# A layer with PEER experts: when the expert rows are fetched, and into which buffers

## The chip, the cores and the metric

The kernel runs on one core of a Trainium2 chip, in one launch. The metric is the device time of that launch in microseconds (us), lower is better. Three runs of the kernel before gave 1982.49, 1975.41 and 1972.63 us, a median of 1975.41. The profiled execution took 1973.37 us, of which the profile's span is 1971.6.

## The reference, cut to what matters

One transformer layer over 512 latent tokens of width 1024 (with 256 context tokens as extra keys): modulated norm, projections, latent attention beside a convolution module, gates, an output projection; then modulated norm and the PEER experts, a residual and a last norm. The part that this change is about:

```python
q = (xc @ w_pq).reshape(P_CHUNK, P_HEADS, 2, P_DK // 2)        # 8 heads
s = jnp.einsum('thpd,hpkd->thpk', q, sub_keys)
s_top, i_top = lax.top_k(s, P_TOPK)                            # 16 of 128 keys, twice
...
expert = e1 * N_KEYS + e2                                      # 16 experts a head, of 16384
gate = jax.nn.softmax(best, axis=-1)
act = jax.nn.gelu(jnp.einsum('thkd,td->thk', u_tab[expert], xc))
return jnp.einsum('thk,thkd->td', gate * act, v_tab[expert])
```

So each token uses 8 x 16 = 128 rows of 1024 numbers from a table u, and 128 rows from a table v.

## The kernel before, in words

The 512 tokens are four tiles of 128, in two groups: tiles 0 and 1, and tiles 2 and 3. The groups go through the layer one after the other, and the experts of the two groups are computed in different ways.

**Group 0 gathers its rows.** For tile q (tile 0) and tile r (tile 1), `expert_in` (line 702) fetches one u row for each of the 128 tokens, 128 x 4 KB = 512 KB, by an indirect DMA that POOL issues (line 704), and DVE multiplies it with the tokens and sums (line 707). There are 128 such calls a tile; below, a *u row* is one such 128-token fetch. When all 128 products of q are there, `expert_mid` (line 724) applies gelu on ACT and the gates on DVE and has PE transpose weights and indices (lines 731, 732). Then `expert_out` (line 737) handles q's v rows in 32 *v groups*: four fetches of 512 KB each (line 748), and eight matmuls that accumulate in PSUM (line 753). For tile r the v rows are summed on DVE instead (`expert_sum`, lines 764 and 770).

**Group 1 computes all 16384 experts densely.** `dense` (from line 843) goes through 64 steps. A step loads two blocks of u and two of v (4 x 512 KB, by SP's DMA queue), splits each into a high and a low part (ACT line 94, DVE line 95), multiplies (PE lines 115 to 117), applies gelu once (ACT line 859) and the scattered gates (DVE line 862). Every eight blocks or so it loads a piece of the gates (`gr`).

**The two are interleaved.** `gathers` (line 774) lists group 0's calls in one fixed order: 128 u rows of q, the `expert_mid` of q, 48 u rows of r (NU = 48), 26 v groups of q, the other 80 u rows of r, the `expert_mid` of r, the last 6 v groups of q (LATE = 6), and 128 sums of r. While group 1 runs, `beside` (line 791) is called at fixed places and takes from that list at a fixed rate: 3.5 rows a unit of the second attention, 6 a column of the second merge (8 columns), 2 a chunk of its output projection, 6 a head of the second route, 0.4 a piece of the scatter of the gates, 4.1 a dense step. A v group counts as four rows. The stages of group 1 in the profile are, in us from the start of the span: second attention about 600 to 740, second merge 740 to 893, its output projection to 919, second route about 920 to 1070, scatter 1070 to 1184, dense 1184 to 1950.

**Buffers.** Every fetched row has a buffer of 4 KB a partition in the pool `gp`, tag `g`, six buffers. POOL issues its fetches in program order and each waits until the last reader of its buffer is done (DVE for a u row, PE for a v row), so six rows at most are on the way or unread. The tile framework orders each engine's instructions as the calls come, with small moves, and gives a buffer to a new tile only when the old tile's last reader stands earlier in the program.

**An idle piece.** `hh` (line 132) holds the modulated activations as a high part `hb0` and a low part `hb1`, each 8 KB a partition. The second group uses only the first (`hb[:1]`, lines 980 and 991), so the low part lies idle from then on.

The lines that decide which call waits for which buffer:

```python
g = gp.tile([P, D], F32, name="g", tag="g")        # expert_in, expert_out, expert_sum; GPB = 6
todo += us[:NU] + vs + us[NU:]                     # gathers: 48 u rows, 26 v groups, 80 u rows
todo += [(4, expert_out, q, i) for i in range(32 - LATE, 32)]
```

Of the kernel before, what the change touches and what calls it, by code (L numbers as in the profile page):

```python
# [8 lines left out]
F32 = mybir.dt.float32  # L9
BF16 = mybir.dt.bfloat16  # L10
F32R = mybir.dt.float32r
# [7 lines left out]
P = 128  # L19
D = 1024  # L20
KC = 8
# [24 lines left out]
PIECES, POFF = 1, 1  # L46
QPOS = (0, 0, 0)
GATES, GOFF, GSTEP = 4, 3, 6
LATE, N0, NU = 6, 0, 48

GROUPS = [[0, 1], [2, 3]]
GT = 2 * P
TB = 16
CB = 8
KEPT = (12,)


@with_exitstack
def tile_layer(ctx, tc, a, out):
    nc = tc.nc  # L60
    te, ve, se, ge, sy = nc.tensor, nc.vector, nc.scalar, nc.gpsimd, nc.sync
# [7 lines left out]
    ep = early.enter_context(tc.tile_pool(name="ep", bufs=1, side="right"))  # L69
# [58 lines left out]
    ones = consts.tile([P, P], F32)  # L128
    ve.memset(ones, 1.0)

    hb = [ep.tile([P, KC, GT], F32, name=f"hb{i}") for i in range(2)]
    hh = tuple(t.bitcast(F32R) for t in hb)
    ckvT = ep.tile([P, NKV], F32)
    KT = [[ep.tile([P if j else HD, NKV], F32, name=f"KT{i}{j}") for j in range(2)] for i in range(2)]
    rows = dram.tile([4, D], F32, name="rows")
# [1 line left out]
    hTd = dram.tile([P, KC, GT], F32, name="hTd")  # L137
# [128 lines left out]
    for i in range(6):  # L266
        t = big(f"x{i}")
# [3 lines left out]
    with tc.tile_pool(name="tmp0", bufs=1) as t0:  # L271
# [48 lines left out]
        for g, o in enumerate((hh, h2nd)):  # L320
            for q in range(2):
                ks = slice(4 * q, 4 * q + 4)
                v = hT[g][q]
# [50 lines left out]
    def queries(tiles, hx):  # L374

        cqT = sp.tile([P, 2, GT], F32, name="cqT", tag="sgm", bufs=2)
        QT = [[None, None] for _ in tiles]
        return QT, [lambda: query_in(tiles, hx, cqT)] + [lambda hf=hf: query_half(tiles, cqT, QT, hf) for hf in range(2)]
# [320 lines left out]
        ve.tensor_mul(gt, gt, mx[:, :, None].to_broadcast([P, PH, TOPK]))  # L699


    def expert_in(r, s):
        g = gp.tile([P, D], F32, name="g", tag="g")
        ge.indirect_dma_start(out=g, out_offset=None, in_=a["u"],  # L704
                              in_offset=bass.IndirectOffsetOnAxis(ap=r["ei"][:, s:s + 1], axis=0))
        scr = sp.tile([P, D], BF16, name="scu", tag="scu")
        ve.scalar_tensor_tensor(scr, g, 1.0, r["h2"], op0=ALU.mult, op1=ALU.mult, accum_out=r["act"][:, s:s + 1])  # L707
# [30 lines left out]
    def expert_out(r, i):  # L738
        if i == 0:
            r["acc"] = psV.tile([P, D], F32, name="acc")  # L740
        acc = r["acc"]
        z = Wz[i % 2]
        ve.tensor_copy(z[:, :, 31], r["wT"][:, i::32])
        gs = []
        for j in range(4):
            tk = 32 * j + i
            g = gp.tile([P, D], F32, name="g", tag="g")
            ge.indirect_dma_start(out=g, out_offset=None, in_=a["v"],  # L748
                                  in_offset=bass.IndirectOffsetOnAxis(ap=r["iT"][:, tk:tk + 1], axis=0))
            gs.append(g)  # L750
        for c in range(2):
            for j in range(4):
                te.matmul(acc[32 * j:32 * j + 32, 512 * c:512 * c + 512], z[:, j, 31 - i:63 - i],  # L753
                          gs[j][:, 512 * c:512 * c + 512], start=i == 0, stop=i == 31,
                          tile_position=(0, 32 * j))
        if i == 31:
            finish(acc, r["t"], lambda n: gp.tile([P, D], F32, name=n, tag="g"))
# [16 lines left out]
    def gathers(res):  # L774
        q, r = res
        todo = [(1, expert_in, q, s) for s in range(NSLOT)]
        todo.append((0, expert_mid, q))
        us = [(1, expert_in, r, s) for s in range(NSLOT)]
        vs = [(4, expert_out, q, i) for i in range(32 - LATE)]
        todo += vs[:N0]  # L780
        vs = vs[N0:]
        todo += us[:NU] + vs + us[NU:]
        todo.append((0, expert_mid, r, False))
        todo += [(4, expert_out, q, i) for i in range(32 - LATE, 32)]
        todo += [(1, expert_sum, r, s) for s in range(NSLOT)]
        return iter(todo)
# [114 lines left out]
    def back(tiles, x1, natural):  # L901
        h2, h2T, parted = norm2(tiles, x1, natural)
        res = []
        for i, t in enumerate(tiles):
            r = dict(t=t, h2=h2[i] if natural else None, x1=x1[i])
            r["gt"] = sp.tile([P, PH, TOPK], F32, name="gt", tag="gt", bufs=4)
            r["ee"] = sp.tile([P, 2, NSLOT], F32, name="ee", tag="ee", bufs=2)
            if natural:
                r["ef"] = sp.tile([P, NSLOT], F32, name="ef", tag="ef", bufs=2)
                r["ei"] = sp.tile([P, NSLOT], I32, name="ei", tag="ei", bufs=2)  # L910
                r["act"] = sp.tile([P, NSLOT], F32, name="act", tag="act", bufs=2)
            res.append(r)
        return res, h2T, parted
# [38 lines left out]
    QT, qsteps = queries(GROUPS[0], hh)  # L952
# [19 lines left out]
    aT = attention(GROUPS[0], QT, fill)  # L972
    conv.close()
    gp = ctx.enter_context(tc.tile_pool(name="gp", bufs=GPB))
    x1 = merge(GROUPS[0], hh, aT, lambda: conv_norm(y), ready=ready)
    turn["split"] = False
    sy.dma_start(hb[0], hTd)
    y = ep.tile([P, KC, GT], F32, name="y", tag="y")
    sy.dma_start(y, yd)
    QT, qsteps = queries(GROUPS[1], hb[:1])  # L980
    qat = {}
    for q, f in zip(QPOS, qsteps):
        qat.setdefault(q, []).append(f)
# [4 lines left out]
    later = route(res, h2T, 1, qat)  # L988
    sT = conv_norm(y)
    aT = attention(GROUPS[1], QT, {}, True)  # L990
    x1 = merge(GROUPS[1], hb[:1], aT, lambda: sT, later)
    later[-1]()
    full, h2T, parted = back(GROUPS[1], x1, False)
    early.close()
    dn = ctx.enter_context(tc.tile_pool(name="dn", bufs=1, side="right"))
# [91 lines left out]
```

## Time and profile before

| what | value |
|---|---|
| median of three runs | 1975.41 us (1972.63 to 1982.49) |
| profiled execution, its span | 1973.37 us, 1971.6 us |
| PE busy | 1780.3 us, 90% of the span |
| DVE busy | 1554.7 us, 79% |
| ACT, POOL busy | 767.8 us and 766.4 us, 39% each |
| DMA moved | 555.66 MB, 282 GB/s over the span |

The busy shares are averages over stages with different limits, so they are read stage by stage: from the windows of the profile (busy time of each engine, granted clock of PE, DMA share in one stretch), and from what each engine's wait ended with. A row's fetch shows twice: as an instruction of POOL (line 704, 748 or 764), which is only its issue, and as its landing, which the profile counts from the start of that instruction.

### The profile page before, as it was taken

Reading aid. Unit: us, or ns where it says so; the run is one execution under the profiler, and the core shown is the slowest. Engines: PE = TensorE matmul, PEld = TensorE weight load, DVE = VectorE, ACT = ScalarE, POOL = GpSimd, SP = SyncE. Lnnn points to the kernel's source line nnn. Section 1 sums busy time; section 2 is a strip of 40 time slices with the busy share of each in tenths; the row PEclk is TensorE's granted clock in tenths of the full one; section 3 lists DMA queues with packets and bytes.
Section 4 is the critical chain, followed back from the end, with each engine's and each line's share of the span. In section 5 each row is a group of like instructions: output and inputs, shape, how many; then the busy total and the mean of one; then the engine's idle time right before and its main releaser. Section 6 shows DMA issues by size and latency. Waiting matters only on the chain.

```text
span 1971.6 us, 29883 instructions
## 1 busy us (share of the span) xinstructions
PE 1780.3 (90%) x10952; PEld 1426.6 (72%) x10952; DVE 1554.7 (79%) x3122; ACT 767.8 (39%) x1141; POOL 766.4 (39%) x582
## 2 busy tenths in 40 slices
PE   4799999799987998599997889999999998999997
PEld 2767777598775667474652568788888787888986
DVE  4658989755699998886797875498996478989998
ACT  5256564543226550001111344333444344434444
POOL 0000000000045876563236882265561255656660
PEclk8899999999998999799999999999999999999999
DMA  8043333357486889898877669899999899999994
GB/s 326 30 145 121 125 115 103 119 193 269 148 321 224 312 314 399 328 408 307 289 266 267 245 225 309 290 392 400 374 397 347 310 349 368 400 400 384 399 399 156
DMA packets 179010, 555.66 MB, mean 282 GB/s; under 512 B 18984, under 2 KB 49192, under 8 KB 178608
## 3 DMA queue, kind: packets, MB, share of 16 engines
q1 hardware_dynamic: 105136, 285.29, 39.8%
q0 software_dynamic: 73728, 268.47, 36.8%
q8 instruction: 86, 1.41, 0.3%
q14 instruction: 60, 0.49, 0.1%
HBM read 533.23 MB, written 20.46 MB: 281 GB/s over the span
## 4 chain that ended last, share of the span: by engine, by line
PE 53%; DVE 18%; DMA 15%; issue 7%; POOL 4%; ACT 3%; SPq 0%; DVEq 0%; ACTq 0%; POOLq 0%
PE ps L116 11%; PE ps L115 11%; PE ps L117 11%; DMA g<-in_u_dram,ei 5%; DMA u<-in_ut_dram 4%; PE ps L113 3%; PE ps L472 3%; PE acc L753 3%; DMA g<-in_v_dram,iT 3%; DVE scu L707 2%; POOL ohC L823 2%; DMA v<-in_v_dram 2%; DVE vsum L770 2%; PE ps L497 2%; PE acc L163 2%
## 5 line engine op out<-in xcount | busy, mean ns | idle before, releaser
L704 POOL DMA_INDIRECT g<-in_u_dram,ei x256 | 347.8, 1358 | 754.0 <-DVE tk L637 539.3
L707 DVE SCALAR_TENSOR_TENSOR scu<-g,h 128x1024 bf16<-128x1024 f32 x256 | 312.2, 1220 | 38.4 <-DMA g<-in_u_dram,ei 36.2
L115 PE MATMUL ps<-h2hi,wp 128*128 128x256 f32 x1024 | 290.9, 284 | 0.0
L117 PE MATMUL ps<-h2hi,wp 128*128 128x256 f32 x1024 | 289.6, 283 | 0.0
L116 PE MATMUL ps<-h2lo,wp 128*128 128x256 f32 x1024 | 289.6, 283 | 0.0
L764 POOL DMA_INDIRECT g<-in_v_dram,ei x128 | 208.1, 1626 | 145.2 <-DVE vsum L770 116.4
L94 ACT CAST wp<-u 128x1024 fp32r<-128x1024 f32 x128 | 134.3, 1049 | 284.0 <-DMA u<-in_ut_dram 171.3
L748 POOL DMA_INDIRECT g<-in_v_dram,iT x128 | 132.7, 1037 | 255.3 <-PE acc L753 218.5
L95 DVE TENSOR_TENSOR wp<-u,wp 128x1024 fp32r<-128x1024 f32 x128 | 156.3, 1222 | 88.7 <-ACT wp L94 87.9
L115 PE MATMUL ps<-v,wp 128*128 128x512 f32 x512 | 203.8, 398 | 14.1 <-ACT v L94 10.2
L116 PE MATMUL ps<-v,wp 128*128 128x512 f32 x512 | 204.8, 400 | 7.9 <-DVE v L95 7.6
L115 PEld LDWEIGHTS ps<-h2hi,wp 128*128 128x128 f32 x1024 | 195.9, 191 | 12.8 <-issue 10.9
L117 PE MATMUL ps<-v,wp 128*128 128x512 f32 x512 | 203.5, 397 | 0.3
L116 PEld LDWEIGHTS ps<-h2lo,wp 128*128 128x128 f32 x1024 | 196.1, 191 | 1.8
L117 PEld LDWEIGHTS ps<-h2hi,wp 128*128 128x128 f32 x1024 | 196.0, 191 | 0.1
L212 DVE SCALAR_TENSOR_TENSOR yo<-glu,cvw,yo 128x512 f32<-128x512 f32 x232 | 172.7, 748 | 4.3 <-ACT yo L210 0.9
L95 DVE TENSOR_TENSOR v<-v 128x1024 fp32r<-128x1024 f32 x128 | 156.3, 1221 | 23.0 <-ACT v L94 23.0
L770 DVE SCALAR_TENSOR_TENSOR vsum<-g,act,vsum 128x1024 f32<-128x1024 f32 x127 | 162.7, 1281 | 0.8
L94 ACT CAST v<-v 128x1024 fp32r<-128x1024 f32 x128 | 132.3, 1044 | 45.9 <-PE ps L116 39.8
L115 PEld LDWEIGHTS ps<-v,wp 128*128 128x128 f32 x512 | 98.4, 192 | 33.9 <-ACT v L94 10.6
L116 PEld LDWEIGHTS ps<-v,wp 128*128 128x128 f32 x512 | 98.3, 192 | 31.6 <-DVE v L95 12.2
L753 PE MATMUL acc<-g,Wz 128*32 128x512 f32 x512 | 102.5, 626 | 19.0 <-DMA g<-in_v_dram,iT 14.0
(305 smaller groups left out, 3642.1 us busy)
## 6 DMA issues: line engine op xcount, KB each, us to landing
v<-in_v_dram SPq DMA_DIRECT2D x128, 512.0 KB, 9.0
u<-in_ut_dram SPq DMA_DIRECT2D x128, 512.0 KB, 8.2
wm<-in_wmod_dram SPq DMA_DIRECT2D x48, 512.0 KB, 5.0
wt<-in_w_pq_dram SPq DMA_DIRECT2D x32, 512.0 KB, 4.1
Gd<-gb SPq DMA_DIRECT2D x16, 928.0 KB, 3.7
gr<-Gd SPq DMA_DIRECT2D x14, 1024.0 KB, 10.8
wt<-in_w_ga_dram SPq DMA_DIRECT2D x16, 512.0 KB, 4.7
wt<-in_w_gc_dram SPq DMA_DIRECT2D x16, 512.0 KB, 4.3
```

What stands on the lines that cost most here:

```text
L94: se.copy(h, raw)
L95: ve.tensor_sub(l, raw, h)
L115: te.matmul(o, w[0], x[0], start=start, stop=False)
L116: te.matmul(o, w[0], x[1], start=False, stop=False)
L117: te.matmul(o, w[1], x[0], start=False, stop=stop)
L212: ve.scalar_tensor_tensor(yo, glu[:, w:w + SEQ], cvw[:, m, w:w + 1], yo, op0=ALU.mult, op1=ALU.add)
L704: ge.indirect_dma_start(out=g, out_offset=None, in_=a["u"], in_offset=bass.IndirectOffsetOnAxis(ap=r["ei"][:, s:s + 1], axis=0))
L707: ve.scalar_tensor_tensor(scr, g, 1.0, r["h2"], op0=ALU.mult, op1=ALU.mult, accum_out=r["act"][:, s:s + 1])
L748: ge.indirect_dma_start(out=g, out_offset=None, in_=a["v"], in_offset=bass.IndirectOffsetOnAxis(ap=r["iT"][:, tk:tk + 1], axis=0))
L753: te.matmul(acc[32 * j:32 * j + 32, 512 * c:512 * c + 512], z[:, j, 31 - i:63 - i], gs[j][:, 512 * c:512 * c + 512], start=i == 0, stop=i ...
L764: ge.indirect_dma_start(out=g, out_offset=None, in_=a["v"], in_offset=bass.IndirectOffsetOnAxis(ap=r["ei"][:, s:s + 1], axis=0))
L770: ve.scalar_tensor_tensor(r["sum"], g, w, r["sum"], op0=ALU.mult, op1=ALU.add)
```

## The change

Four edits go together.

1. The list in `gathers` is reordered: 128 u rows of q, 12 u rows of r, the `expert_mid` of q, 12 more u rows of r, 26 v groups, the other 104 u rows of r; the rest as before. MID = 12 and NU = 24 are places in that list.
2. `expert_out` for group i issues the four fetches of group i + 1, not its own (the first call issues those of 0 and 1), and then the matmuls of group i.
3. The low part of `hh` becomes two tiles of 4 KB a partition with the tag `hl` (class `Halves` lets the old code index them as one).
4. `gtile` gives every fourth row one of the two `hl` buffers, until `home["hl"]` is set to False just before the second `back`, that is at the end of the second merge; from then on all rows are in the six buffers of `gp`, since the memory of the `hl` tiles is given up there (`early.close()`).

```diff
-LATE, N0, NU = 6, 0, 48
+LATE, MID, NU = 6, 12, 24
...
+class Halves:
+    def __init__(self, tiles):
+        self.tiles = tiles
+    def __getitem__(self, i):
+        p, k, *more = i
+        if isinstance(k, slice):
+            return self.tiles[k.start // 4][(p, slice(None), *more)]
+        return self.tiles[k // 4][(p, k % 4, *more)]
...
-    hb = [ep.tile([P, KC, GT], F32, name=f"hb{i}") for i in range(2)]
-    hh = tuple(t.bitcast(F32R) for t in hb)
+    hb = ep.tile([P, KC, GT], F32, name="hb")
+    hh = (hb.bitcast(F32R), Halves([ep.tile([P, 4, GT], F32, name="hl", tag="hl", bufs=2).bitcast(F32R) for _ in range(2)]))
...
+    home = {"n": 0, "hl": True}
+    def gtile():
+        home["n"] += 1
+        if home["hl"] and home["n"] % 4 == 0:
+            return ep.tile([P, D], F32, name="g", tag="hl", bufs=2)
+        return gp.tile([P, D], F32, name="g", tag="g")
     def expert_in(r, s):
-        g = gp.tile([P, D], F32, name="g", tag="g")
+        g = gtile()
...
-        gs = []
-        for j in range(4):
-            tk = 32 * j + i
-            g = gp.tile([P, D], F32, name="g", tag="g")
-            ge.indirect_dma_start(out=g, out_offset=None, in_=a["v"],
-                                  in_offset=bass.IndirectOffsetOnAxis(ap=r["iT"][:, tk:tk + 1], axis=0))
-            gs.append(g)
+        for n in ((0, 1) if i == 0 else (i + 1,)):
+            r["gs", n] = []
+            for j in range(4 if n < 32 else 0):
+                tk = 32 * j + n
+                g = gtile()
+                ge.indirect_dma_start(out=g, out_offset=None, in_=a["v"],
+                                      in_offset=bass.IndirectOffsetOnAxis(ap=r["iT"][:, tk:tk + 1], axis=0))
+                r["gs", n].append(g)
+        gs = r.pop(("gs", i))
...
-        todo.append((0, expert_mid, q))
-        todo += vs[:N0]
-        vs = vs[N0:]
-        todo += us[:NU] + vs + us[NU:]
+        todo += us[:MID] + [(0, expert_mid, q)] + us[MID:NU] + vs + us[NU:]
...
     later[-1]()
+    home["hl"] = False
     full, h2T, parted = back(GROUPS[1], x1, False)
     early.close()
```

Three places show how it moves instructions. The names: `g` is a fetched row, `ei` and `iT` the indices for u rows and v groups, `ohC` a piece of the scatter, `scu` the product of a u row, `hw` the gated activations of a dense step, `wp<-u` and `v<-v` the low parts of the loaded blocks, `Wz` the weights of a v group.

POOL, from the end of the scatter to the end of the program, before:

```order
L823 TENSOR_SCALAR ohC<-iota,tT 128x128 x21
L748 DMA g<-in_v_dram,iT 128x1024 x22
L704 DMA g<-in_u_dram,ei 128x1024 x80
L748 DMA g<-in_v_dram,iT 128x1024 x24
L764 DMA g<-in_v_dram,ei 128x1024 x128
```

and in the change:

```order
L844 TENSOR_SCALAR ohC<-iota,tT 128x128 x21
L771 DMA g<-in_v_dram,iT 128x1024 x2
L726 DMA g<-in_u_dram,ei 128x1024 x104
L771 DMA g<-in_v_dram,iT 128x1024 x20
L788 DMA g<-in_v_dram,ei 128x1024 x128
```

Twenty v fetches that stood here moved ahead, and 24 u rows moved here; of the last six v groups, which need 24 fetches, four fetches now stand ahead of the 104 u rows.

DVE, one and a bit dense steps in the middle of the u rows, before:

```order
L862 TENSOR_TENSOR hw<-hw,gr 128x256 x2
L95 TENSOR_TENSOR wp<-u,wp 128x1024
L95 TENSOR_TENSOR v<-v 128x1024
L95 TENSOR_TENSOR wp<-hw,wp 128x512
L707 SCALAR_TENSOR_TENSOR scu,act<-g,h_4310 128x1024
L95 TENSOR_TENSOR v<-v 128x1024
L707 SCALAR_TENSOR_TENSOR scu,act<-g,h_4310 128x1024 x2
L95 TENSOR_TENSOR wp<-u,wp 128x1024
```

and in the change:

```order
L883 TENSOR_TENSOR hw<-hw,gr 128x256 x2
L729 SCALAR_TENSOR_TENSOR scu,act<-g,h_4311 128x1024
L108 TENSOR_TENSOR v<-v 128x1024
L108 TENSOR_TENSOR wp<-hw,wp 128x512
L729 SCALAR_TENSOR_TENSOR scu,act<-g,h_4311 128x1024
L108 TENSOR_TENSOR v<-v 128x1024
L729 SCALAR_TENSOR_TENSOR scu,act<-g,h_4311 128x1024
L108 TENSOR_TENSOR wp<-u,wp 128x1024
L729 SCALAR_TENSOR_TENSOR scu,act<-g,h_4311 128x1024
L108 TENSOR_TENSOR wp<-u,wp 128x1024
```

Four products a step now stand singly between the step's own work. Counted by the pairs of `hw` rows on DVE, the 80 products before stand in steps 8 to 24 and the 104 of the change in steps 2 to 28; the four v groups after them stand at the same steps (28 to 31) in both, and so does the first sum of r (step 33).

PE, second merge, around the transposes of `act` and `ef` for q, before:

```order
L645 MATMUL ps_6688<-sub_4334,qk 128x128 x2
L731 MATMUL ps_6728<-ident,act 128x128
L732 MATMUL ps_6728<-ident,ef 128x128
L113 MATMUL ps_6748<-hb_90,wt 128x256 x16
L113 MATMUL ps_6770<-ah,wt 128x256 x8
L113 MATMUL ps_6770<-sT,wt 128x256 x8
```

and in the change:

```order
L658 MATMUL ps_6895<-sub_4336,qk 128x128 x2
L753 MATMUL ps_6935<-ident,act 128x128
L754 MATMUL ps_6935<-ident,ef 128x128
L126 MATMUL ps_6955<-hb,wt 128x256 x16
L126 MATMUL ps_6977<-ah,wt 128x256 x8
L126 MATMUL ps_6977<-sT,wt 128x256 x8
L658 MATMUL ps_7001<-sub_4336,qk 128x128 x2
L777 MATMUL acc<-g,Wz_113 32x512
L126 MATMUL ps_7064<-hb,wt 128x256 x16
```

The transposes stand two merge columns later: after the fifth of the eight columns, before after the third. The first v group now stands inside the merge, and in PE's order eight v groups are complete ahead of the second group's last norm, where before there was one.

## Rows read from the trace of the kernel before

**Rows 1.** The page: span and instructions of the profiled execution

```profile
span 1971.6 us, 29883 instructions
```

**Rows 2.** Windows: length, busy us PE, PEld, DVE, ACT, POOL; clock, DMA share, GB/s

```profile
739.70:785.70 46.00, 40.13 (x180) 34.69 (x178) 37.64 (x99) 2.54 (x5) 29.57 (x26) 0.93 1.02 399
...
785.70:807.60 21.90, 0.06 (x2) 0.01 (x1) 21.05 (x67) 3.25 (x4) 9.37 (x9) 0.58 0.71 250
...
807.60:892.70 85.10, 78.08 (x344) 66.85 (x345) 72.70 (x212) 4.48 (x9) 52.95 (x42) 0.95 1.00 394
...
920.00:1070.00 150.00, 129.12 (x586) 68.69 (x576) 111.87 (x556) 28.37 (x51) 59.01 (x59) 0.94 0.79 279
...
1030.00:1070.00 40.00, 28.80 (x106) 8.78 (x105) 25.32 (x114) 4.52 (x9) 19.36 (x20) 0.91 0.81 287
...
1191.20:1284.10 92.90, 92.90 (x618) 74.16 (x617) 45.96 (x61) 36.45 (x44) 28.38 (x28) 1.00 0.90 312
...
1284.10:1485.20 201.10, 191.19 (x1173) 170.87 (x1172) 184.04 (x266) 80.77 (x97) 125.19 (x80) 0.97 1.03 392
...
1191.20:1514.60 323.40, 313.49 (x1986) 272.29 (x1985) 248.48 (x350) 132.80 (x159) 155.37 (x108) 0.98 0.99 368
```

**Rows 3.** Timeline of PE, second merge: start, length, what, idle before

```profile
754.16 9.26 PE L113 MATMUL ps<-hb,wt 128*128 128x256 f32 x32 [5.41 <-DVE sgm L562]
...
807.59 0.47 PE L731 MATMUL ps<-ident,act 128*128 128x128 f32 x1 [21.84 <-DVE act L727]
...
827.29 7.17 PE L113 MATMUL ps<-hb,wt 128*128 128x256 f32 x32 [2.35 <-DVE sgm L562]
...
883.57 5.41 PE L113 MATMUL ps<-ah,wt 128*128 128x256 f32 x16 [3.27 <-DVE sgm L562]
...
892.72 26.77 PE L113 MATMUL ps<-wt,mT 128*128 128x512 f32 x62
```

**Rows 4.** Line 707 (DVE row products) in 739.7 to 919.4: its waits

```profile
  DMA g<-in_u_dram,ei: 21.3, 34
```

**Rows 5.** Line 859 (one gelu per dense step) in 1191 to 1515

```profile
L859 ACT ACTIVATE hw<-ps x27: 583/591/595, 1191.2 to 1514.5; 128x512 f32<-128x512 f32 x27
```

**Rows 6.** Timeline, dense part: DVE row product, then POOL's next row issue

```profile
1299.67 1.22 DVE L707 SCALAR_TENSOR_TENSOR scu<-g,h 128x1024 bf16<-128x1024 f32 x1
...
1300.81 0.08 DVE L707 DVE_READ_ACCUMULATOR scu<-g,h 128x1 f32 x1
...
1301.16 1.81 POOL L704 DMA_INDIRECT g<-in_u_dram,ei  x1 [0.59 <-DVE scu L707]
```

**Rows 7.** Line 748 (v rows), dense stretch 1184 to 1284: issue and landing

```profile
L748 POOL DMA_INDIRECT g<-in_v_dram,iT x22: 946/952/1025, 1197.9 to 1265.5; - x22
...
DMA to landing us min/median/max: 5.8/6.8/8.1
```

**Rows 8.** Line 748 (v rows), second route, 920 to 1070: landing

```profile
DMA to landing us min/median/max: 4.0/5.7/10.0
```

**Rows 9.** Line 704 (u rows), dense stretch 1284 to 1486: issue and landing

```profile
L704 POOL DMA_INDIRECT g<-in_u_dram,ei x75: 949/1692/1991, 1282.7 to 1471.9; - x75
...
DMA to landing us min/median/max: 7.5/9.2/12.7
```

**Rows 10.** Line 704, the one row issued at 1277.1: landing

```profile
DMA to landing us min/median/max: 4.0/4.0/4.0
```

**Rows 11.** Timeline of PE: one v group among the dense matmuls

```profile
1195.40 0.39 PE L117 MATMUL ps<-v,wp 128*128 128x512 f32 x1
...
1195.72 1.92 PE L753 MATMUL acc<-g,Wz 128*32 128x512 f32 x16
...
1197.58 0.38 PE L115 MATMUL ps<-h2hi,wp 128*128 128x256 f32 x1
```

**Rows 12.** Line 753 (v group matmuls), 920 to 1070: what PE waited for

```profile
  DMA g<-in_v_dram,iT: 41.5, 28
```

More of the change, by code (lines that the diff above doesn't have):

```diff
@@ L976, in tile_layer @@
     turn["split"] = False
-    sy.dma_start(hb[0], hTd)
+    sy.dma_start(hb, hTd)
     y = ep.tile([P, KC, GT], F32, name="y", tag="y")
     sy.dma_start(y, yd)
-    QT, qsteps = queries(GROUPS[1], hb[:1])
+    QT, qsteps = queries(GROUPS[1], (hb,))
     qat = {}
@@ L990, in tile_layer @@
     aT = attention(GROUPS[1], QT, {}, True)
-    x1 = merge(GROUPS[1], hb[:1], aT, lambda: sT, later)
+    x1 = merge(GROUPS[1], (hb,), aT, lambda: sT, later)
     later[-1]()
+    home["hl"] = False
     full, h2T, parted = back(GROUPS[1], x1, False)
```

## The prediction, made before the changed kernel was run

> **What bounds the kernel now.** I read the windows by stage first, since the span of 1971.6 us [rows 1] is a chain of stages with different limits, then the waits in the two stages that the change touches.
>
> In the second merge PE is the engine that the others wait for, with gaps: 40.1 of 46.0 us busy, then a stretch of 21.9 us with nothing on PE, then 78.1 of 85.1 [rows 2]. The reader is to see that the stretch is one wait: PE stood 21.84 us at the transpose of `act` [rows 3], because the `expert_mid` of q stood in PE's order before DVE had finished q's 128 products. Three smaller waits follow DVE (5.41, 2.35, 3.27). DVE itself is 82 to 96% busy there (37.6 of 46.0, 21.1 of 21.9, 72.7 of 85.1) and waits 21.3 us for rows that have not landed [rows 4].
>
> In the dense part PE is full where v groups run beside it (92.9 of 92.9 us, DMA share 0.90, 312 GB/s) and nearly full where u rows do (191.2 of 201.1 us, DVE 184.0, DMA share 1.03 at 392 GB/s) [rows 2]. There POOL keeps six rows in flight, and hardly anybody waits for one: rows take 7.5 to 12.7 us to land [rows 9], and it costs nothing because DVE is still busy with the rows before. That cover is six buffers deep, and it is what decides this change.
>
> **The change part by part.** The sum is made against the profiled execution's 1973.4 us; the median shown, 1975.4, is 2 above it.
>
> *Dense u rows: two buffers instead of six.* By the new `expert_out`, the call for group 25 issues the four fetches of group 26. That call is the last ahead of the 104 u rows, and group 26's matmuls come only after them. POOL's order shows it: 20 v fetches after the u rows, where the last six groups need 24. By then `home["hl"]` is False and the lent pair is gone. So four of the six buffers hold rows that nobody reads for the whole of the u rows, and 104 rows pass through the other two. Row n can be issued only when DVE has finished row n - 2, and DVE, in program order, waits for row n with everything queued behind it: the low parts of u and v for the dense matmuls, and through them PE. Nothing else covers the wait.
>
> One turn of the two buffers is: landing of a row, counted from POOL's start, plus the product (1.22 us) and its accumulator read, plus the step to POOL's next issue. The last three are 1.5 us together (1299.67 to 1301.16, [rows 6]). So a turn is L + 1.5, it serves two rows, and 104 rows are 52 turns.
>
> The landing L with two rows in flight is not in the trace of before, so it is bounded. Below: the only row that went out after a pause landed in 4.0 us [rows 10], and the second route has a median of 5.7 at 279 GB/s [rows 2, 8]. Above: 9.2, the median with up to six in flight at 392 GB/s [rows 9]. Between them the dense stretch with bursts of four has 6.8 at 312 GB/s [rows 7]. The changed stretch has the same loads as that one, spread over a longer step, and fewer rows at a time, so it lies between 5.7 and 6.8; POOL's issue itself is longer beside u rows (median 1.69 us against 0.95, [rows 7, 9]), which is inside L. I take 6.5.
>
> The Trainium skill, "DMA: Bandwidth & Descriptors", section "Anatomy of one DMA — SWDGE (gpsimd) path", gives such a fetch about 2 us fixed plus its bytes at 436 GB/s, which for 512 KB is 3.2 us, an estimate from that page; the turn would be 4.7 us and the rows would be hidden (the first rival). The trace does not agree where other loads run: no landing in the rows is under 4.0.
>
> The Trainium skill, "SBUF — State Buffer", section "SBUF: two separate sides", says that POOL cannot write the descriptors of its DMA while a DVE operation holds their shared port; POOL's 1.69 us beside DVE-heavy u rows, and 0.95 beside v groups, agree. By that rule L falls somewhat as DVE waits more, which is within the range.
>
> With 6.5 a turn is 8.0 us and the 104 rows take 52 x 8.0 = 416 us, four rows a step, 26 steps of 16 us. Those are the same 26 steps (2 to 28) that took 323.4 us before [rows 2, 5], 27 gelus with 26 intervals. Cost: 416 - 323 = +93 us. It breaks even at a turn of 323.4 / 52 = 6.2 us, that is L = 4.7. The moved v groups are in this figure: six of them leave the 26 steps, and the u rows that come instead are paid by the turns. After step 28 the orders are alike, so nothing is counted.
>
> Ends for the range: L = 5.4 gives 52 x 6.9 = 359, +36; L = 8.0 gives 494, +171; the full 9.2 gives 556, +233.
>
> *The wait at the transposes.* The last five merge columns are 78.1 us of PE [rows 2], 15.6 each; two columns later is 31 us of PE work, and the wait was 21.84, so it goes. What is late next: in the merge and output projection PE gets seven more v groups, each 1.86 us (1195.72 to 1197.58, [rows 11]), 13 us. Net 21.8 - 13 = 9 us saved at most by PE. DVE loses 24 products (24 x 1.22 = 29 us) there and can keep up. But the v groups now wait on rows inside PE's order, and DMA is at 394 to 399 GB/s in this stage [rows 2], so not all of it arrives. I take -7, between +5 and -20 (the whole wait, should the groups fit in PE's other gaps).
>
> *A group ahead, eight buffers.* While group 1's attention and merge run, eight rows instead of six may be out. DVE's 21.3 us of waits for rows [rows 4] is what that could shorten, and it is in the figure above. In the second route PE waits 41.5 us (weight loads and matmuls counted each) for v rows [rows 12]; but there the lent pair is gone, and with six buffers POOL could already issue half a group ahead, so issuing it earlier in the program changes what POOL waits for little. In the scatter POOL's own order has 21 fetches instead of 23. Together -6, between +5 and -20.
>
> *The low part as two tiles* has the same bytes, and the class only indexes them: 0.
>
> Sum: 1973.4 + 93 - 7 - 6 = 2053 us.
>
> **The rivals.**
>
> *The rows are hidden anyway (faster).* If a lone row lands in 4.0 us [rows 10], a turn is 5.5 and 52 turns 286 us, less than PE needs: its 313.5 us in those steps [rows 2] less six groups at 1.86 is 302. Then the dense part gains 21, and with the two gains the sum is 1973 - 21 - 13 = 1939. For it: that landing. Against it: it is one row, in a pause, and no stage with loads of u and v beside has a median under 5.7. It decides below L = 4.7.
>
> *A draw.* L near 4.7 to 5.2 lets the turn cost about what the other two edits bring: 52 x 6.45 = 335, +12, and the sum is about 1972. For it: in the route the quickest are 4.0 and the median only 5.7. Against it: the dense part loads 2 MB a step beside the rows.
>
> *The wait also takes PE's clock.* With a 16 us step PE has 302 / 26 = 11.6 us of work and stands for the rest. PE's granted clock was 0.58 in the stretch where it stood 21.8 us, and 0.91 where it was busy 28.8 of 40.0 us [rows 2]; pieces at the lower of its two levels (1.2 GHz) would follow each pause. If the whole stretch went to that level, PE's 302 us would become 604 and the rows would no longer be the bound: +281, 2241. Against it: 0.91 at 72% busy says that only pieces fall, and at 0.9 PE needs 335 us, less than 416.
>
> *Landings stay long.* If rows beside the dense loads keep the 9.2 us of [rows 9] with two in flight, +233: about 2193. For it: loads of u and v come in bursts. Against it: those 9.2 us are with three and more rows queued ahead.
>
> **How the numbers follow.** A difference under 0.5% (10 us) can't be told from no change. Forecast, two buffers set the pace, 1990 to 2135: 0.78. Long landings or the clock, over 2135: 0.12. Draw: 0.05. Hidden and faster: 0.05. The range of the forecast takes L from 5.4 (1973 + 36 - 20 = 1989) to 8.0 (1973 + 171 - 9 = 2135). The likeliest is 2053. Faster by over 0.5%: 0.06; within: 0.04; slower: 0.90.
>
> **What would show it.** Right: on DVE, the u products of the dense part wait for rows, some 1.5 to 3 us each, and this is the largest wait of DVE; POOL's issues of u rows there each wait for the product two rows before; steps 2 to 28 take about 416 us; PE's busy share there falls to about 302 / 416 = 73%; PE has no long wait at the transposes of `act`; the part after step 28 takes as long as before. Wrong: if the dense u rows run at 12 to 13 us a step, L is what I mis-sized; if more than two u rows are in flight there, my reading of the buffers is wrong; if the added time lies in the merge or route, the v groups in PE's order are the cause.

## The result, and the profile after

The changed kernel takes 2067.2 us (median of four runs, 2060.3 to 2075.4) against 1974.0 for the kernel before on the same chip: a ratio of 1.047, with a 95% interval of 1.043 to 1.050. That is slower, as forecast, and 14 us above the forecast of 2053. The profiled execution took 2060.3 us. Its page, beside [rows 1] (span, busy time by engine, then the chain of work that ended last, by its largest members):

```profile
span 2058.4 us, 29893 instructions
...
PE 1814.3 (88%) x10952; PEld 1434.9 (70%) x10952; DVE 1560.7 (76%) x3122; ACT 765.5 (37%) x1141; POOL 781.0 (38%) x582
...
DMA g<-in_u_dram,ei 15%; PE ps L129 7%; PE ps L130 7%; PE ps L128 7%; PE ps L126 4%; PE ps L485 3%; DMA g<-in_v_dram,iT 3%; PE acc L777 3%; POOL ohC L844 3%; PE ps L510 2%; DVE scu L729 2%; PE acc L176 2%; DVE vsum L794 2%; DMA v<-in_v_dram 2%; POOL g L788 1%
```

The span is 86.8 us longer. A landing of u rows is now the largest member of the chain, 15% of the span. Line numbers have moved: u rows are issued at line 726 (704 before) and multiplied at 729 (707), v groups are fetched at 771 (748) and multiplied at 777 (753), the transpose of `act` is at 753 (731), `Wz` is written at 765.

The windows of the change, with the columns of [rows 2]. First from the first merge column to the end of the output projection, then from gelu 2 to gelu 28 of the dense part, from 28 to 29, and from 29 to the end:

```profile
729.60:922.10 192.50, 162.91 (x733) 120.03 (x732) 132.77 (x415) 14.34 (x24) 101.51 (x87) 0.94 0.92 351
1197.40:1589.60 392.20, 333.88 (x1891) 280.76 (x1890) 269.23 (x376) 130.64 (x158) 164.08 (x101) 0.94 0.83 289
1589.60:1614.90 25.30, 20.23 (x109) 14.28 (x108) 16.40 (x25) 5.29 (x8) 12.45 (x10) 0.97 0.78 274
1614.90:2058.40 443.50, 420.96 (x2623) 368.81 (x2622) 378.52 (x397) 189.76 (x229) 221.05 (x143) 0.97 0.94 356
```

Two windows of the kernel before for the same places (merge with its output projection, and gelu 2 to gelu 29):

```profile
732.60:919.50 186.90, 152.16 (x637) 119.27 (x640) 157.66 (x455) 14.34 (x24) 107.00 (x87) 0.91 0.95 367
1191.20:1527.80 336.60, 326.69 (x2074) 282.81 (x2073) 254.74 (x358) 137.94 (x164) 159.18 (x112) 0.98 0.98 363
```

So the span's 86.8 us are made up like this: gelu 2 to 29 takes 417.5 us instead of 336.6 (+80.9); merge and output projection 192.5 instead of 186.9 (+5.6); the merge begins 3.0 earlier; from the end of the output projection to gelu 2 it is 275.3 instead of 271.7 (+3.6); after gelu 29 it is 443.5 instead of 443.8 (-0.3).

What waits for what in the dense u rows: the waits of DVE and of POOL from gelu 2 to 29 (instruction, what it waited for, us in total, times, longest):

```profile
DVE scu L729 <- DMA g<-in_u_dram,ei: 126.1, 93, 6.4
DVE wp L108 <- ACT wp L107: 4.8, 2, 3.7
```

```profile
POOL g L726 <- DVE scu L729: 223.7, 100, 7.1
```

In the kernel before, the same wait of DVE was 10.7 us, four times. The order of events shows in the timelines of DVE and of POOL over four rows (start, duration, instruction, and in brackets the idle time before it and what ended it):

```profile
1331.23 1.22 DVE L729 SCALAR_TENSOR_TENSOR scu<-g,h 128x1024 bf16<-128x1024 f32 x1 [1.49 <-DMA g<-in_u_dram,ei]
1332.38 0.08 DVE L729 DVE_READ_ACCUMULATOR scu<-g,h 128x1 f32 x1
1332.38 1.22 DVE L108 TENSOR_TENSOR wp<-u,wp 128x1024 fp32r<-128x1024 f32 x1
...
1338.30 1.23 DVE L729 SCALAR_TENSOR_TENSOR scu<-g,h 128x1024 bf16<-128x1024 f32 x1 [0.73 <-DMA g<-in_u_dram,ei]
1339.45 0.08 DVE L729 DVE_READ_ACCUMULATOR scu<-g,h 128x1 f32 x1
1339.45 1.22 DVE L108 TENSOR_TENSOR v<-v 128x1024 fp32r<-128x1024 f32 x1
```

```profile
1328.87 1.69 POOL L726 DMA_INDIRECT g<-in_u_dram,ei  x1 [4.13 <-DVE scu L729]
1332.73 1.69 POOL L726 DMA_INDIRECT g<-in_u_dram,ei  x1 [2.17 <-DVE scu L729]
1336.10 1.69 POOL L726 DMA_INDIRECT g<-in_u_dram,ei  x1 [1.68 <-DVE scu L729]
1339.80 1.69 POOL L726 DMA_INDIRECT g<-in_u_dram,ei  x1 [2.02 <-DVE scu L729]
```

The row whose product starts at 1338.30 went out at 1332.73, 5.6 us earlier, right behind the product of 1331.23. Between the two lies one other row (issued at 1328.87, multiplied at 1334.59). So two rows circulate; the step from a product's end to the next issue is as short as before [rows 6], but it now serves the row two places on. All of the 104 rows, with their landing counted from the start of the issue, beside [rows 9]:

```profile
L726 POOL DMA_INDIRECT g<-in_u_dram,ei x104: 944/1690/1699, 1206.7 to 1606.6; - x104
...
DMA to landing us min/median/max: 4.2/5.7/9.7
```

From 1206.7 to 1606.6 are 103 intervals of 3.88 us, that is 7.77 us a turn of two rows.

In the merge, the two long waits of PE on its timeline, beside [rows 3], and the waits of DVE beside [rows 4]:

```profile
778.56 5.22 PE L126 MATMUL ps<-ah,wt 128*128 128x256 f32 x16 [10.18 <-DVE sgm L575]
...
832.03 0.45 PE L753 MATMUL ps<-ident,act 128*128 128x128 f32 x1 [14.29 <-DVE act L749]
```

```profile
DVE Wz L765 <- PE acc L777: 22.5, 3, 8.7
DVE sgm L575 <- PE ps L126: 16.6, 2, 10.6
DVE scu L729 <- DMA g<-in_u_dram,ei: 13.3, 19, 2.1
```

PE still stands 14.3 us at the transposes, and DVE has a new wait: it writes the weights `Wz` of a v group, which has two tiles, and stands until PE has done the v group before last. That is a wait for PE, and none of PE's own waits in this stage is put down to `Wz`.

### The profile page after: what moved, and what is told of

Same layout as the page of the kernel before. It is cut to its first block, busy times and chain, and to the rows that moved or that the text cites. A ratio compares the mean times of both kernels' runs of the same rounds, so it can differ in the third digit from the quotient of the medians.

```text
span 2058.4 us, 29893 instructions
## 1 busy us (share of the span) xinstructions
PE 1814.3 (88%) x10952; PEld 1434.9 (70%) x10952; DVE 1560.7 (76%) x3122; ACT 765.5 (37%) x1141; POOL 781.0 (38%) x582
## 4 chain that ended last, share of the span: by engine, by line
PE 41%; DMA 23%; DVE 14%; issue 13%; POOL 6%; ACT 2%; SPq 0%; DVEq 0%; POOLq 0%; ACTq 0%
DMA g<-in_u_dram,ei 15%; PE ps L129 7%; PE ps L130 7%; PE ps L128 7%; PE ps L126 4%; PE ps L485 3%; DMA g<-in_v_dram,iT 3%; PE acc L777 3%; POOL ohC L844 3%; PE ps L510 2%; DVE scu L729 2%; PE acc L176 2%; DVE vsum L794 2%; DMA v<-in_v_dram 2%; POOL g L788 1%
## 5 line engine op out<-in xcount | busy, mean ns | idle before, releaser
L726 POOL DMA_INDIRECT g<-in_u_dram,ei x256 | 366.3, 1431 | 874.9 <-DVE tk L650 538.5
L129 PE MATMUL ps<-v,wp 128*128 128x512 f32 x512 | 214.4, 419 | 45.6 <-DVE v L108 45.2
L128 PE MATMUL ps<-v,wp 128*128 128x512 f32 x512 | 212.3, 415 | 23.1 <-ACT wp L107 17.0
L130 PE MATMUL ps<-v,wp 128*128 128x512 f32 x512 | 212.1, 414 | 2.4
L129 PEld LDWEIGHTS ps<-v,wp 128*128 128x128 f32 x512 | 101.8, 199 | 82.0 <-DVE v L108 61.8
L107 ACT CAST wp<-hw 128x512 fp32r<-128x512 f32 x64 | 39.7, 620 | 262.4 <-DVE hw L883 262.4
L777 PE MATMUL acc<-g,Wz 128*32 128x512 f32 x512 | 108.4, 640 | 29.6 <-DMA g<-in_v_dram,iT 28.4
```

The lines of the kernel that those rows point to most:

```text
L107: se.copy(h, raw)
L128: te.matmul(o, w[0], x[0], start=start, stop=False)
L129: te.matmul(o, w[0], x[1], start=False, stop=False)
L130: te.matmul(o, w[1], x[0], start=False, stop=stop)
L726: ge.indirect_dma_start(out=g, out_offset=None, in_=a["u"], in_offset=bass.IndirectOffsetOnAxis(ap=r["ei"][:, s:s + 1], axis=0))
```

## The experiments

The theory was the forecast's: the four held rows leave two buffers, whose turns set the pace of the u rows. The rivals were the new order itself (24 more dense u rows, v groups among the merge's matmuls) and a row that takes a fixed time of some queue. Ratios are to the kernel before, run on the same chip, with a 95% interval.

**Nothing held.** The table of fetches in `expert_out`, with HOLD = 0 (the experiments with none, three and five rows held differ from the change in this table alone):

```diff
-        for n in ((0, 1) if i == 0 else (i + 1,)):
-            r["gs", n] = []
-            for j in range(4 if n < 32 else 0):
+        ahead = {0: ((0, 0, 4), (1, 0, 4)), 31 - LATE: ((32 - LATE, 0, HOLD),),
+                 32 - LATE: ((32 - LATE, HOLD, 4), (33 - LATE, 0, 4)), 31: ()}
+        for n, lo, hi in ahead.get(i, ((i + 1, 0, 4),)):
+            r.setdefault(("gs", n), [])
+            for j in range(lo, hi):
```

> The change, but the call for group 25 fetches nothing ahead; group 26 is fetched with group 27 by the next call, after the 104 u rows. Theory (two buffers set the pace of the u rows): with all six buffers free the rows are hidden behind PE again, gelus 2 to 29 of the dense part take about 337 us as in the kernel before instead of 417.5, and the time falls by 81 to about 1980 us (1970 to 1990). Rival (the order itself costs: 104 u rows instead of 80 and v groups among the merge's matmuls): the dense part stays near 400 us and the time at 2050 to 2070.

Measured: 1981.6 us, ratio 0.9996 (0.9972 to 1.0020). The window from gelu 2 to 29 and DVE's waits in it:

```profile
1210.67:1539.10 328.43, 315.81 (x1980) 282.14 (x1981) 276.38 (x393) 137.60 (x165) 166.71 (x108) 0.98 0.98 369
```

```profile
DVE scu L730 <- DMA g<-in_u_dram,ei: 11.5, 5, 3.6
```

The hold was the whole loss: without it the other edits together come out at the kernel before. 102 of the 104 rows go out at 2.6 us each again (1197.3 to 1460.7; the first two go out in the scatter). The stretch is even 8 us shorter than before: six v groups have left it, and PE is busy 315.8 us there instead of 326.7. The rival that blames the order for the dense part is out.

**Three rows held instead of four** (HOLD = 3).

> The change, but only three of the four rows of group 26 are held through the u rows, so three buffers serve them. Theory (turns of the buffers): 104 / 3 = 34.7 turns of a landing plus 1.5 us; with a landing between the 5.8 us seen with two in flight and the 9.2 with six, say 6.7, a turn is 8.2 and the rows take 284 us, less than PE's work, so nearly all of the 81 us is gone: 1980 to 1995. Rival (a row takes 3.77 us of some engine or queue, 392 us for 104, whatever the number of buffers): no change, 2050 to 2070.

Measured: 2024.3 us, 1.021 (1.016 to 1.025): between the two expectations. The issues of the rows and what POOL waited for, then DVE's wait from gelu 2 to 29:

```profile
L727 POOL DMA_INDIRECT g<-in_u_dram,ei x104: 950/1692/1978, 1214.0 to 1531.1; - x104
...
  DVE scu L730: 155.3, 85
```

```profile
DVE scu L730 <- DMA g<-in_u_dram,ei: 70.6, 42, 4.4
```

103 intervals in 317.1 us are 3.08 us a row, a turn of three rows 9.24, where I expected 8.2. POOL's issues now follow the product three rows before. So the pace does depend on the number of buffers, and the fixed time a row is out; but the third buffer brought less than expected. From issue to product a row took 7.6 us (median), against 5.9 with two. The landing is not what I had wrong: it was 6.7 us in the median of the 76 rows whose landing this trace holds whole, as I had assumed (5.7 with two in flight). What I left out is that a landed row now often stands behind DVE's other work, 0.9 us on average in these rows, and DVE waits before 42 products only.

**The hold in the kernel before**, whose dense u rows are 80:

```diff
-        gs = []
-        for j in range(4):
-            tk = 32 * j + i
+        for n in {31 - LATE: (i, i + 1), 32 - LATE: ()}.get(i, (i,)):
+            r["gs", n] = []
+            for j in range(4):
+                tk = 32 * j + n
...
+        gs = r.pop(("gs", i))
```

> The kernel before with one edit: the call for group 25 also fetches group 26, so four of six buffers are held through its 80 dense u rows. Theory (two buffers): 40 turns of 7.5 us are 300 us where the 80 rows took about 241 to 250, so +50 to +60: about 2030 (2015 to 2045). Rival (a hold costs only together with the new order, whose u rows are more): within 10 us of the kernel before, 1974.

Measured: 2056.3 us, 1.038 (1.034 to 1.043). The hold alone makes the old kernel slow, so neither the order nor the lent pair is needed for it. My size was too small:

```profile
L704 POOL DMA_INDIRECT g<-in_u_dram,ei x80: 947/1689/1702, 1287.5 to 1598.2; - x80
```

That is 3.93 us a row, 7.87 a turn, 311 us in all. Before, the same 80 rows went out in 205 us (1266.8 to 1471.9) and not in the 241 I had taken, and they were done 42 us ahead of gelu 29. All but 2 us of that lead went first; on the other hand the u rows start 13 us later after gelu 2. The stretch from gelu 2 to 29 is 73 us longer (409.7 instead of 336.6), and that is the loss.

**Five rows held** (group 26 and the first row of group 27), a single run; the table against that of the first experiment:

```diff
-        ahead = {0: ((0, 0, 4), (1, 0, 4)), 31 - LATE: ((32 - LATE, 0, HOLD),),
-                 32 - LATE: ((32 - LATE, HOLD, 4), (33 - LATE, 0, 4)), 31: ()}
+        ahead = {0: ((0, 0, 4), (1, 0, 4)), 31 - LATE: ((32 - LATE, 0, 4), (33 - LATE, 0, 1)),
+                 32 - LATE: ((33 - LATE, 1, 4),), 31: ()}
```

> The change, but the call for group 25 fetches group 26 and the first row of group 27, so five of six buffers are held through the 104 u rows and one serves them all. Theory (turns of the buffers, a landing set mostly by what else is in flight): with one u row at a time the landing falls from the 5.8 us seen with two to between 4.2 and 5.3, a turn is 5.7 to 6.8, 104 turns are 590 to 705 us, and the time is 2260 to 2370. Rival (a landing of 5.8 us that does not depend on the rows in flight): a turn of 7.3, 760 us, 2420 to 2430. Rival (a row takes a fixed 3.9 us of a queue): no change, 2067.

Measured: 2116.2 us, under the first two ranges, because the hold did not stay to the end. POOL in the held part, and the matmuls of group 26 on PE:

```profile
1327.94 1.69 POOL L726 DMA_INDIRECT g<-in_u_dram,ei  x1 [5.45 <-DVE scu L729]
1335.27 1.16 POOL L726 DMA_INDIRECT g<-in_u_dram,ei  x1 [5.64 <-DVE scu L729]
1341.41 1.69 POOL L726 DMA_INDIRECT g<-in_u_dram,ei  x1 [4.97 <-DVE scu L729]
```

```profile
1564.49 1.92 PE L779 MATMUL acc<-g,Wz 128*32 128x512 f32 x16
```

The framework had moved group 26's matmuls ahead, to after 52 rows; from there five rows were in flight. Up to there the rows went one at a time, from 1217.3 to 1572.6 in 51 turns of 6.97 us, with 5.5 us (mean; median 5.7) from issue to product. So a lone row comes hardly sooner than one of two (median 5.9): its turn is a little over the theory's 5.7 to 6.8 us and under the 7.3 of the first rival, and the fixed 3.9 us a row is out here as well.

**The order alone**, in the kernel before:

```diff
-LATE, N0, NU = 6, 0, 48
+LATE, MID, NU = 6, 12, 24
...
-        todo.append((0, expert_mid, q))
...
-        todo += us[:NU] + vs + us[NU:]
+        todo += us[:MID] + [(0, expert_mid, q)] + us[MID:NU] + vs + us[NU:]
```

> The kernel before with the new order alone (the expert_mid of q after 12 u rows of r, 24 ahead of the v groups); own fetches, six buffers everywhere. Theory (as forecast): the wait at the transposes shrinks, the seven v groups that move into the merge cost 13 us of PE, and the dense u rows stay hidden with six buffers: 1960 to 1975. Rival (the v groups in PE's order wait for rows and make the merge and the route later): 1980 to 1995, with the dense part starting later than at 1191 us.

Measured: 1992.3 us, 1.0049 (1.0023 to 1.0075), a little slower. Merge and output projection took 202.7 us (742.1 to 944.8) against 186.9, and from gelu 2 to 29 it was 328.8, 8 less than before. The rival had the right outcome: the order costs in the merge, and part of that comes back in the dense part. Its cause, v groups that wait for rows, is only a part of it: in the merge PE is busy 21.3 us longer (173.5 against 152.2), and all its waits together are 5.5 us shorter, though 8.1 us for v rows are new among them.

**The lent pair alone**, that is the change with order and fetches as before:

```diff
-LATE, MID, NU = 6, 12, 24
+LATE, MID, NU = 6, 0, 48
...
-        for n in ((0, 1) if i == 0 else (i + 1,)):
+        for n in (i,):
...
-            for j in range(4 if n < 32 else 0):
+            for j in range(4):
```

> The kernel before with the lent pair alone: every fourth row in one of the two 4 KB tiles until the end of the second merge; order and fetches as before. Theory (DVE's 21.3 us of waits for rows in the merge shorten with eight buffers, but landings grow since DMA is at 0.95 there): gain of 0 to 8 us, 1966 to 1976. Rival (the lent pair is worth what the new order loses, 10 us or more, since the order alone gave 1992 and the order with the pair 1982): 1960 to 1968.

Measured: 1976.0 us, 0.9992 (0.9968 to 1.0015): no difference. Merge and output projection took 183.9 us. With the new order it is otherwise: the order alone took 1992.3 us, the same order with the lent pair and the fetch ahead, and nothing held, 1981.6 on the same chip (ten runs each), 10.6 us less. In the merge PE waits for v rows with the order alone, and hardly at all with both:

```profile
PE acc L753 <- DMA g<-in_v_dram,iT: 8.1, 3, 5.0
```

```profile
PE acc L780 <- DMA g<-in_v_dram,iT: 0.3, 1, 0.3
```

Which of the two edits does it was not tried.

**Where the v groups stand.** Both kernels are the one with nothing held, with the lent pair and the fetch ahead, and `expert_mid` after 24 u rows; they differ in NU, the u rows ahead of the v groups.

```diff
-LATE, MID, NU = 6, 12, 24
+LATE, MID, NU = 6, 24, 24
```

> As the kernel without held rows (e1_hold0), with the expert_mid of q after 24 u rows of r instead of 12; v groups follow at once. Theory (the wait at the transposes is what is left of the merge's gaps): the wait is under 5 us, the stage from the first merge column to the end of the output projection takes 180 to 187 instead of 193.9, and the time is 1968 to 1978. Rival (v groups in the merge cost more than the transposes): the stage stays over 190 and the time over 1978.

```diff
-LATE, MID, NU = 6, 12, 24
+LATE, MID, NU = 6, 24, 48
```

> No rows held, the lent buffers and the fetch a group ahead as in the change, but the expert_mid of q after 24 u rows of r and the v groups after 48 as in the kernel before, so the transposes stand four merge columns later and no v group stands in the merge. Theory (the merge did not gain because q's 128 products still came late for two columns and because the v groups' matmuls then stood in PE's and DVE's way): first merge column to end of output projection falls from 186.9 us before (192.5 in the change) to 165 to 178, and the time to 1955 to 1970. Rival (the merge is bound by landings or DVE, so the wait only moves elsewhere): the stage stays at 184 to 192 and the time at 1970 to 1985.

Measured: with NU = 24 1977.0 us, 1.0007 (0.9989 to 1.0026), with NU = 48 1968.7 us, 0.9964 (0.9943 to 0.9985). With NU = 24, PE's wait at the transposes, then DVE's at `Wz` (both from the first merge column to the end of the output projection):

```profile
PE ps L754 <- DVE act L750: 3.2, 1, 3.2
```

```profile
DVE Wz L766 <- PE acc L780: 37.5, 5, 13.0
```

With NU = 48, PE's waits in the same stage:

```profile
PE ps L127 <- DVE sgm L576: 11.7, 5, 5.6
...
PE ps L754 <- DVE act L750: 1.3, 1, 1.3
```

At MID = 24 the wait at the transposes is gone in both. With v groups in the merge the stage still takes 193.2 us, as with MID = 12 (193.9); without them it is 174.2. The stage in both, NU = 24 first:

```profile
734.50:927.70 193.20, 175.26 (x734) 120.89 (x732) 131.06 (x415) 14.41 (x24) 97.62 (x87) 0.96 0.91 350
...
731.60:905.80 174.20, 154.66 (x635) 120.05 (x636) 155.29 (x457) 14.38 (x24) 106.15 (x87) 0.94 0.97 378
```

With the v groups PE is busy 20.6 us longer, and all its waits together are no longer (17.9 against 19.5 us). So it was PE's own time for the v groups there that took back what the later transposes gave, and not DVE's wait at `Wz`. With NU = 48 stage and time came as the theory had them; with NU = 24 the wait went and the time fell into the theory's range, but the stage stayed over 190 us, as its rival said.

**Is anything but the place of `expert_mid` needed?** The kernel before with the diff of the order alone, and MID, NU = 24, 48:

> The kernel before with one edit, the expert_mid of q after 24 of the 48 u rows instead of ahead of them; no lent pair, no fetch ahead, no held rows. Theory (the later place of the transposes is what helped in e6_mid24): first merge column to end of output projection 172 to 178 us instead of 186.9, and the time 0.2 to 0.6% under the kernel before, as e6_mid24. Rival (the lent pair and the fetch a group ahead are needed for it): the stage over 182 and no difference to the kernel before.

Measured: 1974.5 us against 1981.9 for the kernel before on the same chip, 0.9964 (0.9946 to 0.9983): 0.4% faster, by that one edit, as the theory had it. Merge and output projection:

```profile
736.80:908.80 172.00, 152.37 (x633) 119.60 (x632) 148.67 (x440) 14.29 (x24) 99.11 (x84) 0.93 0.98 375
```

The same PE work as before (152.4 and 152.2 us) in 172.0 us instead of 186.9. The lent pair and the fetch ahead are not needed for it. Not all of these 15 us stay: from the end of the output projection to gelu 2 this run took 283.8 us, where the kernel before took 271.7, and PE's waits for v rows there are 24.2 us instead of 14.0. Then the version with both of these and a still later `expert_mid` (the edit against MID = 24):

```diff
-LATE, MID, NU = 6, 24, 48
+LATE, MID, NU = 6, 36, 48
```

> As e6_mid24 (nothing held, lent pair, fetch a group ahead, v groups after 48 u rows) with the expert_mid of q after 36 u rows instead of 24. Theory (PE's wait at the transposes is already 1.3 us in e6_mid24, so nothing is left to gain there): the same time as e6_mid24 within 0.3%. Rival (the first v rows, which need the indices from this expert_mid, come late for the route): 5 to 15 us slower than e6_mid24.

Measured: 1970.2 us, 0.9942 (0.9920 to 0.9964), the fastest ratio, though its interval overlaps the two before. Merge and output projection took 161.9 us. PE waited 8.0 us at the first v group, just behind that stage, as the rival has it (the profile puts the end of this wait down to a u product of DVE), and the stretch from there to gelu 2 took 285.2 us; that cost less than the stage gained. The time is 0.2% from that with MID = 24, as the theory has it.

## Why the prediction came out right, and where its steps failed

**Two buffers instead of six: right in kind, some 15% too dear.** DVE's largest wait is the landing of u rows, POOL's issues follow the product two rows before, and taking the hold away takes the whole loss away. The forecast was 52 turns of 8.0 us, 416; measured are 52 of 7.77, 404. Of the two parts of a turn, L was taken too long: 6.5, where the 104 rows have a mean of 6.1 (median 5.7; over many turns it is the mean that adds up). The rest was right: 1.5 us from the start of a product to the issue that waits for it, and 97 of the 104 products start within 0.2 us of the landing of their row. Over the dense part +80.9 us stands against +93. DVE's single waits were 1.4 us (126.1 over 93), a little under the 1.5 to 3 named as a sign. The reading of the place was slightly off too: I had 26 steps, but by the framework's placing the rows run into the step from 28 to 29, which took 25.3 us. That nothing is lost after the rows are through was right (443.5 and 443.8).

The Trainium skill, "DMA: Bandwidth & Descriptors", section "Anatomy of one DMA — SWDGE (gpsimd) path", would have made such a landing 3.2 us, an estimate from its figures, and the rows hidden. The trace does not agree: with two rows in flight the median landing was 5.7 us and the shortest 4.2, and a lone row took 5.7 from issue to product. By the break-even of 4.7 that the forecast worked out, the measurement decides for a loss.

**The transposes: wrong.** I let the 21.84 us go because PE comes two columns later. But the products and the gates of `expert_mid` moved in DVE's order as well: 12 more u products and two columns' work now stand ahead of them there. Counted from the first merge column, PE reached the transposes after 53.2 us before (807.6 - 21.84 - 732.6) and after 88.1 now (832.0 - 14.29 - 729.6); DVE was ready after 75.0 and 102.4. DVE was 27 us later, PE 35 (two columns, and 10.18 us at `sgm` where there were 5.41, [rows 3]). So 7.5 us went, not 21.8. I had named DVE as "can keep up", and that was the step that failed: a thing moved to a later place is later on every engine that has a part in it.

**The v groups in the merge: priced about right here.** I priced them at 13 us of PE's time. In the two profiles PE's busy time in the stage rises by 10.8 us (162.9 against 152.2; the v groups' matmuls are 14.0), and its waits fall by 5.2 (29.6 against 34.7), mostly at the transposes. Net -7 was forecast; +5.6 is what came, because 14 us of the transposes' wait stayed. DVE's wait at `Wz` (22.5 us here, none before) is a wait for PE; that it costs time is not shown. The price isn't fixed: in the two experiments that differ in NU the v groups in the merge cost PE 20.6 us of busy time.

**A group ahead, eight buffers: a gain only with v groups in the merge.** I gave them -6. With the old order the lent pair brings nothing (0.9992), and with `expert_mid` later but no v groups in the merge the two together bring nothing either (0.9964 with and without). With the change's order they bring 10.6 us (1981.6 against 1992.3), and so all edits without the hold come out at 0.9996. In the merge PE's wait for v rows, which that order had brought there, goes from 8.1 us to 0.3, and PE's busy time from 173.5 to 166.8, which is not explained. I had looked for the gain in DVE's waits for u rows. Those fell too, from 21.3 us [rows 4] to 13.3, but to 17.6 with the pair alone, which gained nothing by it. In route and scatter, 3.6 us longer in all, PE waits 22.4 us for v rows where it waited 14.0; the same stretch took 273.3 to 278.6 us in the experiments with none, three and five rows held, which have the same order there.

**The low part as two tiles** was counted at nothing, and nothing in the profiles speaks against it.

So the sum of 2053 stands 7 us under the profiled 2060.3: the small terms came to +6 instead of -13 (5.6 + 3.6 - 3.0 - 0.3), 19 us, less the 12 by which the large one was too dear. That the sum came so near is in part luck, two errors of opposite sign. The median of the runs is another 7 above the profiled one.

**The rivals.** Hidden rows and the draw are out by the landing, 5.7 us in the median and 6.1 in the mean. Long landings are out: 9.2 us was the median with six rows in flight, and it fell with their number. PE's clock did fall a little, 0.94 from gelu 2 to 29 against 0.98, and PE's busy time there rose from 326.7 to 354.1 us (333.88 + 20.23), for 2000 matmuls instead of 2074. PE was therefore busy 85% of the stretch from gelu 2 to 28 and not 73%. I count nothing for it: 404 of the 417.5 us are the turns of the rows, and a turn is landing, product and issue, without a part of PE's. That the clock cost nothing was not tried by itself.

## What to carry to other kernels

A fetch issued a step ahead in the program holds its buffer for everything that stands between the fetch and its reader: where a list changes from one kind of work to another, count the buffers left over for the work between. With N buffers a gather runs at N rows per turn (landing, any wait of the landed row for its reader, product, step to the next issue), as it did here with one, two and three, and N must be large enough for that to beat the engine that is fed. An edit's worth can hang on another's: the lent pair and the fetch ahead gained 10.6 us where v groups stood in the merge, and nothing where they did not. To judge a stage whose wait should go, ask when each engine reaches the new place, not only the one that waited.

## What the runs showed of the hardware

The landing of a 512 KB gather beside the dense loads barely depends on whether it is alone: 5.7 us (median) from issue to product with one row in flight, 5.9 with two, nearly all of it the landing (5.7 with two). Then it grows: 6.7 with three, over the 76 rows whose landing that trace holds whole, and 9.2 with up to six [rows 9]. The traffic grows with it, from 240 GB/s with one to 288, 331 and 392, so that the part of the rows' own number is not told apart. Time per row by free buffers: 6.97 us with one, 3.88 with two, 3.08 with three, 2.6 with six, where the rows no longer set the pace.

POOL's issue of a row took 1.69 us in 96 of the 104 rows of the change, although DVE was idle for a third of the stretch (285.6 of 417.5 us busy). The timelines above show why: a free buffer comes with the end of a product, and DVE's next operation starts in the same instant (1332.38), ahead of the issue (1332.73). In all 96, one of DVE's 1.22 us operations for the low parts of u or v (line 108) had begun 0.35 us before the issue. The other 8 issues took 0.95 us. DVE was at work throughout that time in four of these as well, but in three it began with the short gate products (0.42 us each), and in one the long operation began only 0.03 us before the issue. So not any work of DVE lengthens the issue.

The Trainium skill, "SBUF — State Buffer", section "SBUF: two separate sides", has POOL's descriptor writing held off while DVE has their shared port. The trace agrees as far as that: the issue is 0.7 us longer where the long operation was already running. The forecast's hope that idle time on DVE would shorten the issue, and with it the landing, was not met: the median issue stayed at 1.69 us [rows 9], because it nearly always falls into DVE's busy part.
